# Other token widths in the last gate and the first mixer, and a one-instruction final scaling, in a two-layer hybrid trunk

## The chip, the cores and the metric

The kernel runs on one core of a Trainium2 chip. Its time is that of one execution on the device, in microseconds (us). The core's engines are named as in the profile: PE is TensorE (PEld is its weight loads, which overlap its products), DVE is VectorE, ACT is ScalarE, POOL is GpSimd, SP is SyncE, which issues nearly all DMAs. Every engine runs its instructions in order and waits on semaphores for what other engines produce.

## What is computed

The reference is one inference step of a trunk of two layers over 1024 prompt tokens and 8 sample tokens, 1032 in all, with 1024 features. Layer 0 mixes tokens with a convolution module, layer 1 with a chunked state-space scan; both have a feed-forward part and a gate:

```python
for i in range(DEPTH):
    u = rmsnorm(h, g_mix[i])
    o = conformer_mixer(u, ...) if i % 2 == 0 else mamba2_mixer(u, ...)
    h = h + o
    h = h + swiglu(rmsnorm(h, g_ffn[i]), ffn_w_gate[i], ffn_w_up[i], ffn_w_down[i])
    gate = jax.nn.sigmoid(rmsnorm(h, g_ple[i]) @ ple_w_gate[i])
    h = h + (p[i] @ ple_w_proj[i]) * gate
return rmsnorm(h, g_final), ...
```

The conformer mixer begins with `u @ w_pw1` (1024 x 2048), a sigmoid gate between its two halves, and a convolution over 31 tokens. The parts of interest here are that first product, at the kernel's start, and the second layer's `gate` with the final `rmsnorm`, at its end.

## The kernel before

Features lie on the 128 partitions, so that a tensor of 1024 features is 8 tiles `h[m]` of 128 x 1032 tokens. Every product is exact to about 32-bit: an operand is split into a high and a low part (`split`: ACT writes the high part in the matmul's fp32r type, DVE the difference), and one product of a 128-wide slice is three matmuls (`mm3`, lines 132 to 134), each with a weight load of its own. `product` (line 136) runs 8 slices, thus 24 matmuls, into one bank of PSUM. A bank holds 512 columns, so the 1032 tokens are cut into blocks, `BLK = ((0, 388), (388, 386), (774, 258))`, offset and width. PE has seven banks for such products (tag `mm`).

At the start, SP loads weights and inputs in an order written out by hand: the embedding's inputs `p` block by block (`ple_load`), the vectors, `x` block 0 (`load_x`), the weights of the first mixer product, then blocks 1 and 2 of `x`. PE first runs half of the embedding products of layer 0 (`ple_products`), meanwhile ACT and DVE split `x` (`ready`); then `pw1(m)` runs for each of 8 feature tiles two products per block, `a` and `b`. ACT copies the embedding products out of PSUM (`pstg`, line 250), which frees their banks.

At the end, `ple(1, ...)` runs the gate of layer 1 through `grouped`: tiles m = 0 and 1 for all three blocks, then tiles 2 to 7 for all three blocks, so that the weights of six tiles stay in place. After each product, `emit` does on DVE a multiplication by the norm factor (`t`, line 526), on ACT the sigmoid (527), on DVE a multiplication by the embedding product `pj` (528) and the addition to `h` (529), on ACT the square of `h` (204), on DVE its addition to `stat` (205). When a block has all 8 tiles, `norm.finish` sums over the partitions with a matmul (214, for the very last square 216), takes a root on ACT (219) and a reciprocal on DVE (220); then `after1` scales the 8 tiles by `g_final` and the norm factor and stores them. In blocks 0 and 1 a tile is scaled by ACT (line 1396) and then by POOL (1397); in the last block tiles 0, 2 and 4 likewise (1400, 1401) and the other five by one DVE instruction (1403). The last block's tiles are stored two by two, in four DMAs.

The order on each engine is not quite that of the code: a scheduler moves instructions within what their dependencies allow, when the program is built. Engines then follow that order.

Of the kernel before, what the change touches and what calls it, by code (L numbers as in the profile page):

```python
# [16 lines left out]
P = 128  # L17
# [8 lines left out]
NG = 8  # L26
PH = SEQ // 8 + 1
BLK = ((0, 388), (388, 386), (774, 258))
BLQ = tuple((T // 4 * b, T // 4) for b in range(4))
HT = T // 2  # L30
QT = T // 4
# [26 lines left out]
def trunk_kernel(ctx: ExitStack, tc: tile.TileContext, I, O):  # L58
# [172 lines left out]
                               op0=ALU.mult, op1=ALU.mult)  # L231
        split(t[:, :n], uh[:, o:o + n], ul[:, o:o + n], eng=eng)

    def ple_load(i, pt, stage, blocks=BLK, ks=(0, 1)):
        for o, n in blocks:
            for k in ks:
                raw = stage(k, o, n)
                nc.sync.dma_start(out=raw, in_=I["p"][i, k, :, o:o + n])
                split(raw, pt[k][0][:, o:o + n], pt[k][1][:, o:o + n])

    def ple_products(pool, ps, i, pt, tag, halves=(0, 1), w=None):
        for s in halves:
            w = w or kview(slab(I["w_proj"][i, s], 1024), 2)
            for mm in range(4):
                m = 4 * s + mm
                stg = pool.tile([P, T], F32, name="pstg", tag=tag, bufs=3 if tag == "v" else 2)
                for o, n in BLK:
                    a = ps.tile([P, 512], F32, name="a", tag="mm")
                    product(a[:, :n], w, mm * P, pt, o, n)
                    S.activation(out=stg[:, o:o + n], in_=a[:, :n], func=AF.Copy)  # L250
                nc.scalar.dma_start(out=proj_d[i][m], in_=stg)
                yield
            w = None
# [247 lines left out]
                    later(4, lambda o=o, n=n: norm.finish(o, n))  # L501
        return h, hs, u, norm.rstd

    def grouped(xp, weight, emit, after, cut=4):
        for ms in (range(cut), range(cut, KT)):
            ws = {}
            for o, n in BLK:
                for m in ms:
                    if o == 0:
                        ws[m] = kview(slab(weight(m), 1024, xp if m - ms[0] >= 2 else None, len(ms) - 2), KT)  # L510
                    emit(m, ws[m], o, n)
                    tick()
                if cut in ms:
                    after(o, n)

    def ple(i, h, nu, rstd2, ps, after):
        with tc.tile_pool(name=f"pleg{i}", bufs=2, reuse_waits="tile") as pool:
            norm = Norm(ps)

            def emit(m, w, o, n):  # L520
                pj = pool.tile([P, 388], F32, name="pj", tag="pj", bufs=3)
                nc.sync.dma_start(out=pj[:, :n], in_=proj_d[i][m, :, o:o + n])
                a = ps.tile([P, 512], F32, name="a", tag="mm")
                product(a[:, :n], w, 0, nu, o, n)
                t = pool.tile([P, 388], F32, name="t", tag="t", bufs=3)
                V.tensor_tensor(out=t[:, :n], in0=a[:, :n], in1=rstd2[:, o:o + n], op=ALU.mult)
                x = S.activation(out=t[:, :n], in_=t[:, :n], func=AF.Sigmoid)
                V.tensor_tensor(out=t[:, :n], in0=t[:, :n], in1=pj[:, :n], op=ALU.mult)
                V.tensor_tensor(out=h[m][:, o:o + n], in0=h[m][:, o:o + n], in1=t[:, :n], op=ALU.add)
                if o != BLK[-1][0] or m < KT - 1:  # L530
                    norm.add(h[m][:, o:o + n], o, n, V)
                else:
                    behind(S.activation(out=warm[:, :1], in_=warm[:, 1:], func=AF.Sqrt), x, norm.squared)
                    norm.add_last(h[m][:, o:o + n], n)

            def done(o, n):
                def run():
                    norm.finish(o, n)
                    after(norm.rstd, o, n)
                later(1, run)  # L540

            grouped(pool, lambda m: I["w_pgate"][i, m], emit, done, 2)

    l1a = None

# [7 lines left out]
    with tc.tile_pool(name="l0", bufs=2, reuse_waits="tile") as pool:  # L553
# [8 lines left out]
                norm.add(h[m][:, o:o + n], o, n, V)  # L562

        def ready(b):
            o, n = BLK[b]
            for m in range(KT):
                if b in SCALED_LATER:
                    split(h[m][:, o:o + n], U[m][0][:, o:o + n], U[m][1][:, o:o + n], scale=col("g_mix", m))
                else:
                    scaled_split(h[m], col("g_mix", m), norm.rstd, U[m], o, n)  # L570
# [4 lines left out]
        with tc.tile_pool(name="ple0", bufs=2, reuse_waits="tile") as pp:  # L575
            pt = [(pp.tile([P, T], F32R, name="ph", tag="ph"), pp.tile([P, T], F32R, name="pl", tag="pl"))
                  for _ in range(2)]
            praw = [pp.tile([P, T], F32, name="praw", tag="praw") for _ in range(2)]
            w0 = [wp.tile([P, 1024], F32, name="wraw", tag="wraw")] + \
                [pp.tile([P, 1024], F32R, name=f"w{x}", bufs=1) for x in "hl"]  # L580
            for k in range(2):
                hf = slice(512 * k, 512 * k + 512)
                nc.sync.dma_start(out=w0[0][:, hf], in_=I["w_proj"][0, 0, :, hf])
                split(*(t[:, hf] for t in w0))
                ple_load(0, pt, lambda k, o, n: praw[k][:, o:o + n], BLK[:1], (k,))
            ple_load(0, pt, lambda k, o, n: praw[k][:, o:o + n], BLK[1:])
            nc.sync.dma_start(out=vec, in_=I["vec"])
            load_x(*BLK[0])
            w1 = pw1_weights(0)
            for b in BLK[1:]:  # L590
                load_x(*b)
            for _ in ple_products(pp, ps, 0, pt, "pstg", (0,), kview(w0[1:], 2)):
                pass
            squares(*BLK[0])
            if 0 not in SCALED_LATER:
                norm.finish(*BLK[0])
            ready(0)

        cs = pool.tile([P, T], F32, name="cs", tag="cs", bufs=1)
# [4 lines left out]
        with tc.tile_pool(name="conv", bufs=2, reuse_waits="tile") as cp:  # L604
            def pw1(m, out, w=None):
                wa, wg = w or pw1_weights(m)
                v = cp.tile([P, T], F32, name="v", tag="v", bufs=3)
                out.append(v)
                for i, (o, n) in enumerate(BLK):
                    a = ps.tile([P, 512], F32, name="a", tag="mm")  # L610
                    product(a[:, :n], wa, 0, U, o, n)
                    b = ps.tile([P, 512], F32, name="b", tag="mm")
                    product(b[:, :n], wg, 0, U, o, n)
                    if i in SCALED_LATER:
                        r = norm.rstd[:, o:o + n]
                        s = pool.tile([P, 388], F32, name="s", tag="s")
                        V.tensor_tensor(out=s[:, :n], in0=b[:, :n], in1=r, op=ALU.mult)
                        t = pool.tile([P, 388], F32, name="t", tag="t")
                        V.tensor_tensor(out=t[:, :n], in0=a[:, :n], in1=r, op=ALU.mult)
                    else:  # L620
                        s, t = b, a
                    g = s if i in SCALED_LATER else pool.tile([P, 388], F32, name="s", tag="s")
                    S.activation(out=g[:, :n], in_=s[:, :n], func=AF.Sigmoid, bias=col("b_pw1", KT + m))
                    V.scalar_tensor_tensor(out=v[:, o:o + n], in0=t[:, :n], scalar=col("b_pw1", m), in1=g[:, :n],
                                           op0=ALU.add, op1=ALU.mult)
                    yield
# [77 lines left out]
            vs = []  # L704
            it = pw1(0, vs, w1)
            if 0 in SCALED_LATER:
                norm.finish(*BLK[0])
            for b in (1, 2):
                squares(*BLK[b])
                if b in SCALED_LATER:  # L710
                    ready(b)
                    next(it)
                    norm.finish(*BLK[b])
                else:
                    next(it)
                    norm.finish(*BLK[b])
                    ready(b)
            nc.sync.dma_start(out=st, in_=I["conv_state"])
            nc.sync.dma_start(out=cmask, in_=I["cmask"])
# [180 lines left out]
    def win(i):  # L900
        return kview(slab(I["w_in"][i], 1024), KT)

    ple(0, h, U, rstd, ps, after0)
    its = [in_proj(win(16 + ct), raw, cst[:, ct, :, 3], AF.Copy, 3) for ct, raw in zip((16, 24), raws)]
    for it in its:
        for _ in range(2):
# [444 lines left out]
    with tc.tile_pool(name="ps2", bufs=7, space=PSUM, reuse_waits="tile") as ps:  # L1351
# [35 lines left out]
        l1.close()  # L1387
        h, hp, u, rstd = ffn(1, entry, ps, xs)

        out = ctx.enter_context(tc.tile_pool(name="out", bufs=1)).tile([P, KT, BLK[-1][1]], F32, name="out")  # L1390

        def after1(rstd, o, n):
            for m in range(KT):
                hx, g, r = h[m][:, o:o + n], col("g_final", m), rstd[:, o:o + n]
                if o != BLK[-1][0]:
                    S.activation(out=hx, in_=hx, func=AF.Copy, scale=g)
                    G.tensor_tensor(out=hx, in0=hx, in1=r, op=ALU.mult)
                    nc.sync.dma_start(out=O["y"][m, :, o:o + n], in_=hx)
                elif m in (0, 2, 4):
                    S.activation(out=hx, in_=hx, func=AF.Copy, scale=g)  # L1400
                    G.tensor_tensor(out=out[:, m], in0=hx, in1=r, op=ALU.mult)
                else:
                    V.scalar_tensor_tensor(out=out[:, m], in0=hx, scalar=g, in1=r, op0=ALU.mult, op1=ALU.mult)
                if o == BLK[-1][0] and m % 2 == 1:
                    nc.sync.dma_start(out=O["y"][m - 1:m + 1, :, o:o + n].rearrange("m p n -> p m n"),
                                        in_=out[:, m - 1:m + 1])

        ple(1, h, u, rstd, ps, after1)
        flush()
        hp.close()  # L1410

# [125 lines left out]
```

## Time and profile before

| what | us |
|---|---|
| three runs | 3060.24, 3068.0, 3070.94 |
| their median | 3068.0 |
| the profiled execution | 3064.59 |
| its span, first to last instruction | 3062.8 |

The span is cut into times from its start. In the rows below, a timeline row gives an instruction's start, its duration, engine, line, what it writes and reads with partitions x columns, and in brackets how long its engine sat idle before it and what ended the idle time. A matmul's shown duration is longer than the distance to the next one, since matmuls are pipelined; what one costs PE is the distance between the starts.

### The profile page before, as it was taken

What the parts mean: (1) busy time and instruction counts of PE and PEld (TensorE: products, weight loads), DVE (VectorE), ACT (ScalarE), POOL (GpSimd) and SP (SyncE); (2) the same over time, 40 slices, a digit from 0 to 9 for tenths busy, and PEclk for the clock granted to TensorE, in tenths of its full rate; (3) what the DMA queues carried; (4) which work ended last, traced back from release to release, by engine and by line L of the source; (5) the groups of instructions that cost most, each with busy time, mean ns of one, the idle gap of its engine ahead of it and who ended that gap; (6) DMA issues with size and microseconds to landing.
All of it is one profiled execution on the core that took longest, in us unless ns stands there. A gap on an engine that the chain in (4) does not pass through costs nothing.

```text
span 3062.8 us, 51428 instructions
## 1 busy us (share of the span) xinstructions
PE 2933.8 (96%) x20613; PEld 2887.0 (94%) x20613; DVE 1971.8 (64%) x3206; ACT 1410.8 (46%) x2542; POOL 542.6 (18%) x540
## 2 busy tenths in 40 slices
PE   9999999999999999999999999999989999999997
PEld 8998889999999999899888998888889999999997
DVE  7787795555444478476687667865495555444476
ACT  6226653333321155666667676733353333321164
POOL 0001310000000021144454444531200000000022
PEclk9999999999999999999999999999999999999998
DMA  5336532222252233223334333566522222252222
GB/s 184 79 87 210 164 97 86 84 77 80 73 194 84 66 103 112 64 96 96 83 104 105 94 88 92 141 190 161 165 94 80 74 83 83 70 187 83 67 82 94
DMA packets 198063, 325.91 MB, mean 106 GB/s; under 512 B 50240, under 2 KB 120256, under 8 KB 197824
## 3 DMA queue, kind: packets, MB, share of 16 engines
q1 hardware_dynamic: 195520, 314.17, 33.4%
q10 hardware_dynamic: 2304, 8.46, 0.7%
q8 instruction: 162, 2.65, 0.4%
q14 instruction: 77, 0.63, 0.1%
HBM read 241.59 MB, written 72.58 MB: 103 GB/s over the span
## 4 chain that ended last, share of the span: by engine, by line
PE 73%; DVE 13%; ACT 6%; DMA 4%; issue 3%; POOL 1%; SPq 0%; DVEq 0%; ACTq 0%; POOLq 0%
PE a L134 8%; PE a L133 8%; PE a L132 8%; PE pA L132 5%; PE pA L133 5%; PE pA L134 5%; PE mm L133 4%; PE mm L132 4%; PE mm L134 4%; PE pC L134 3%; PE pC L132 3%; PE pC L133 3%; DVE xf L1024 2%; PE cacc L686 1%; PE pB L133 1%
## 5 line engine op out<-in xcount | busy, mean ns | idle before, releaser
L132 PE MATMUL mm<-u,whi 128*128 128x258 f32 (+2 forms) x1600 | 513.3, 322 | 13.5 <-ACT whi L112 8.8
L133 PE MATMUL mm<-u,whi 128*128 128x258 f32 (+2 forms) x1600 | 516.6, 323 | 0.5 <-DVE u L113 0.5
L134 PE MATMUL mm<-u,wlo 128*128 128x258 f32 (+2 forms) x1600 | 509.5, 320 | 1.6 <-DVE wlo L113 1.5
L112 ACT ACTIVATE whi<-wraw 128x1024 fp32r<-128x1024 f32 (+1 forms) x199 | 207.5, 1044 | 393.7 <-PE a L133 230.4
L205 POOL TENSOR_TENSOR stat<-stat,sq 128x258 f32<-128x258 f32 (+2 forms) x70 | 63.5, 907 | 1451.0 <-ACT sq L204 1445.4
L132 PEld LDWEIGHTS mm<-u,whi 128*128 128x128 f32 x1600 | 304.7, 191 | 16.4 <-ACT whi L112 9.8
L133 PE MATMUL a<-hh,whi 128*128 128x388 f32 (+2 forms) x984 | 316.0, 321 | 0.5 <-DVE hh L113 0.5
L134 PE MATMUL a<-hh,wlo 128*128 128x388 f32 (+2 forms) x984 | 315.6, 322 | 0.0
L132 PE MATMUL a<-hh,whi 128*128 128x388 f32 (+2 forms) x984 | 310.4, 322 | 4.3 <-ACT hh L112 4.3
L133 PEld LDWEIGHTS mm<-u,whi 128*128 128x128 f32 x1600 | 305.7, 191 | 2.6 <-DVE u L113 1.1
L134 PEld LDWEIGHTS mm<-u,wlo 128*128 128x128 f32 x1600 | 304.1, 191 | 3.9 <-DVE wlo L113 2.3
L113 DVE TENSOR_TENSOR wlo<-wraw,whi 128x1024 fp32r<-128x1024 f32 (+1 forms) x199 | 244.1, 1227 | 59.0 <-ACT whi L112 58.0
L474 DVE TENSOR_TENSOR h<-a,h 128x388 f32<-128x388 f32 (+2 forms) x288 | 145.5, 512 | 186.7 <-PE a L134 185.8
L132 PE MATMUL a<-u,whi 128*128 128x258 f32 (+2 forms) x648 | 205.1, 319 | 9.0 <-ACT u L112 6.6
L134 PE MATMUL a<-u,wlo 128*128 128x258 f32 (+2 forms) x648 | 200.8, 313 | 3.5 <-DVE wlo L113 3.5
L133 PE MATMUL a<-u,whi 128*128 128x258 f32 (+2 forms) x648 | 202.6, 314 | 0.0
L132 PEld LDWEIGHTS a<-hh,whi 128*128 128x128 f32 x984 | 185.3, 189 | 4.6 <-ACT hh L112 4.6
L133 PEld LDWEIGHTS a<-hh,whi 128*128 128x128 f32 x984 | 186.3, 189 | 0.8 <-DVE hh L113 0.8
L134 PEld LDWEIGHTS a<-hh,wlo 128*128 128x128 f32 x984 | 186.4, 189 | 0.1
L113 DVE TENSOR_TENSOR wal<-sa,wah 128x1024 fp32r<-128x1024 f32 x44 | 54.4, 1237 | 151.9 <-ACT wah L112 151.9
L132 PEld LDWEIGHTS a<-u,whi 128*128 128x128 f32 x648 | 123.4, 191 | 12.2 <-ACT u L112 7.6
L134 PEld LDWEIGHTS a<-u,wlo 128*128 128x128 f32 x648 | 123.4, 191 | 4.9 <-DVE wlo L113 4.7
(354 smaller groups left out, 8536.5 us busy)
## 6 DMA issues: line engine op xcount, KB each, us to landing
wraw<-in_w_in SPq DMA_DIRECT2D x48, 512.0 KB, 4.6
hid<-hid SPq DMA_DIRECT2D x88, 258.0 KB, 2.4
hraw<-hid SPq DMA_DIRECT2D x44, 516.0 KB, 3.6
wraw<-in_w_gate SPq DMA_DIRECT2D x44, 512.0 KB, 3.3
wraw<-in_w_up SPq DMA_DIRECT2D x44, 512.0 KB, 3.3
wraw<-in_w_pw SPq DMA_DIRECT2D x32, 512.0 KB, 3.5
wraw<-in_w_down SPq DMA_DIRECT2D x32, 512.0 KB, 3.5
am<-ac_d SPq DMA_DIRECT2D x64, 256.0 KB, 3.5
```

What stands on the lines that cost most here:

```text
L112: S.activation(out=hi, in_=raw, func=AF.Copy)
L113: eng.tensor_tensor(out=lo, in0=raw, in1=as32(hi), op=ALU.subtract)
L132: TE.matmul(out, lhsT=wh, rhs=xh, start=start, stop=False, skip_group_check=onto)
L133: TE.matmul(out, lhsT=wh, rhs=xl, start=False, stop=False, skip_group_check=onto)
L134: TE.matmul(out, lhsT=wl, rhs=xh, start=False, stop=stop, skip_group_check=onto)
L205: return eng.tensor_tensor(out=self.acc[:, o:o + n], in0=self.acc[:, o:o + n], in1=sq[:, :n], op=ALU.add)
L474: V.tensor_tensor(out=h[m][:, o:o + n], in0=a[:, :n], in1=h[m][:, o:o + n], op=ALU.add)
L686: TE.matmul(acc[:, j], lhsT=we[:, i], rhs=raw[:, g, 4 - e:132 - e], start=i == 0, stop=i == nb - 1)
L1024: V.scalar_tensor_tensor(out=d, in0=raw[:, j + o:j + o + 512], scalar=col("w_conv", 4 * ct + j), in1=d, op0=ALU.mult, op1=ALU.add)
```

## The change

A second and a third table of widths come beside `BLK`. `BLK0 = 258, 388, 386` is used for everything ahead of the convolution (loads of `x` and `p`, `ple_load`, `ple_products` of both layers, `ready`, `pw1`); `BLKF = 388, 386, 194, 64` for the gate of layer 1, which so has four blocks. In `after1`, all blocks but the last are scaled by one DVE instruction a tile; the last block, now 64 wide, is scaled and stored as before. `BLK` stays everywhere else.

```diff
 BLK = ((0, 388), (388, 386), (774, 258))
+BLK0 = ((0, 258), (258, 388), (646, 386))
+BLKF = ((0, 388), (388, 386), (774, 194), (968, 64))
...
-    def ple_load(i, pt, stage, blocks=BLK, ks=(0, 1)):
+    def ple_load(i, pt, stage, blocks=BLK0, ks=(0, 1)):
...
-                for o, n in BLK:
+                for o, n in BLK0:
                     a = ps.tile([P, 512], F32, name="a", tag="mm")
                     product(a[:, :n], w, mm * P, pt, o, n)
...
-    def grouped(xp, weight, emit, after, cut=4):
+    def grouped(xp, weight, emit, after, cut, blocks):
...
-                if o != BLK[-1][0] or m < KT - 1:
+                if o != blocks[-1][0] or m < KT - 1:
...
-            load_x(*BLK[0])
+            load_x(*BLK0[0])
...
-                for i, (o, n) in enumerate(BLK):
+                for i, (o, n) in enumerate(BLK0):
                     a = ps.tile([P, 512], F32, name="a", tag="mm")
                     product(a[:, :n], wa, 0, U, o, n)
...
-                if o != BLK[-1][0]:
-                    S.activation(out=hx, in_=hx, func=AF.Copy, scale=g)
-                    G.tensor_tensor(out=hx, in0=hx, in1=r, op=ALU.mult)
+                if o != BLKF[-1][0]:
+                    V.scalar_tensor_tensor(out=hx, in0=hx, scalar=g, in1=r, op0=ALU.mult, op1=ALU.mult)
                     nc.sync.dma_start(out=O["y"][m, :, o:o + n], in_=hx)
...
-        ple(1, h, u, rstd, ps, after1)
+        ple(1, h, u, rstd, ps, after1, BLKF)
```

The order moves at three places. First SP's queue at the start: the end of the first block of `x`, the two weight loads of the first mixer product, and the second block. Before:

```order
L558 DMA h_190<-in_x 128x388
L558 DMA h_191<-in_x 128x388
L558 DMA h_192<-in_x 128x388
L126 DMA wraw<-in_w_pw 128x1024 x2
L558 DMA h_185<-in_x 128x386
L558 DMA h_186<-in_x 128x386
```

and now:

```order
L560 DMA h_190<-in_x 128x258
L560 DMA h_191<-in_x 128x258
L560 DMA h_192<-in_x 128x258
L128 DMA wraw<-in_w_pw 128x1024 x2
L560 DMA h_185<-in_x 128x388
L560 DMA h_186<-in_x 128x388
```

The queue's order is the same; the first eight loads are narrower, and what is behind them starts that much sooner.

Second PE's last instructions: the end of the last tile's product, then the two matmuls of the last norm sum (`st`). Before:

```order
L132 MATMUL a<-u,xhi 128x258
L133 MATMUL a<-u,xhi 128x258
L134 MATMUL a<-u,xlo 128x258
L214 MATMUL st<-stat_28816,mean 128x258
L216 MATMUL st<-sq,mean 128x258
```

and now:

```order
L134 MATMUL a<-u,xhi 128x64
L135 MATMUL a<-u,xhi 128x64
L136 MATMUL a<-u,xlo 128x64
L216 MATMUL st<-stat_28816,mean 128x64
L218 MATMUL st<-sq,mean 128x64
```

Eight products of 24 matmuls at 258 columns are now eight at 194 and eight at 64, and a further norm sum, at 194 columns, stands after the 47th of the 64-wide matmuls of tiles 2 to 7.

Third DVE's queue in the block after the 386-wide one, around the reciprocal of that block's norm. Before, with the block's 258-wide evictions around it and the scaling on ACT and POOL:

```order
L529 TENSOR_TENSOR h_28825<-h_28825,t 128x258
L220 RECIPROCAL stat_28817<-stat_28817 128x386
L205 TENSOR_TENSOR stat_28816<-stat_28816,sq 128x258
L526 TENSOR_TENSOR t<-a,stat_28818 128x258
L528 TENSOR_TENSOR t<-t,pj 128x258
```

and now:

```order
L531 TENSOR_TENSOR h_28825<-h_28825,t 128x194
L222 RECIPROCAL stat_28817<-stat_28817 128x386
L207 TENSOR_TENSOR stat_28816<-stat_28816,sq 128x194
L528 TENSOR_TENSOR t<-a,stat_28818 128x194
L1398 SCALAR_TENSOR_TENSOR h_28822<-h_28822,vec,stat_28817 128x386
L1398 SCALAR_TENSOR_TENSOR h_28823<-h_28823,vec,stat_28817 128x386
L1398 SCALAR_TENSOR_TENSOR h_28824<-h_28824,vec,stat_28817 128x386
L1398 SCALAR_TENSOR_TENSOR h_28825<-h_28825,vec,stat_28817 128x386
L1398 SCALAR_TENSOR_TENSOR h_28826<-h_28826,vec,stat_28817 128x386
L1398 SCALAR_TENSOR_TENSOR h_28827<-h_28827,vec,stat_28817 128x386
L1398 SCALAR_TENSOR_TENSOR h_28828<-h_28828,vec,stat_28817 128x386
L1398 SCALAR_TENSOR_TENSOR h_28829<-h_28829,vec,stat_28817 128x386
```

Eight scalings stand in DVE's queue between one tile's `t` and its multiplication by `pj`; they stand so after the reciprocals of the 388-wide and the 194-wide block too.

## Rows read from the trace of the kernel before

**Rows 1.** The page's part 1: busy time, share and instructions of each engine.

```profile
PE 2933.8 (96%) x20613; PEld 2887.0 (94%) x20613; DVE 1971.8 (64%) x3206; ACT 1410.8 (46%) x2542; POOL 542.6 (18%) x540
```

**Rows 2.** Busy time by stretch: length, engines' busy us (instructions), granted clock, DMA, GB/s.

```profile
60.00:80.00 20.00, 20.00 (x148) 20.00 (x147) 19.99 (x39) 7.36 (x12) 0.03 (x1) 1.00 0.38 98
...
200.00:250.00 50.00, 50.00 (x355) 49.99 (x354) 38.06 (x70) 18.31 (x34) 0.12 (x1) 1.00 0.41 116
...
3020.00:3040.00 20.00, 20.00 (x148) 19.73 (x147) 14.04 (x24) 11.14 (x20) 3.91 (x5) 1.00 0.23 73
3040.00:3050.00 10.00, 5.13 (x39) 4.69 (x37) 8.88 (x12) 2.94 (x7) 8.02 (x7) 0.85 0.49 173
3050.00:3063.00 13.00, 1.73 (x4) 0.50 (x2) 6.11 (x8) 2.27 (x5) 2.72 (x3) 0.50 0.24 81
```

**Rows 3.** Timeline of PE in the last gate, some starts.

```profile
2950.44 0.34 PE L132 MATMUL a<-u,whi 128*128 128x388 f32 x1
...
2958.94 0.34 PE L132 MATMUL a<-u,whi 128*128 128x386 f32 x1
...
2967.40 0.60 PE L214 MATMUL st<-stat,mean 128*128 128x258 f32 x2
...
2967.95 0.28 PE L133 MATMUL a<-u,whi 128*128 128x258 f32 x1
...
2973.61 0.34 PE L132 MATMUL a<-u,whi 128*128 128x388 f32 x1
2973.79 0.33 PE L133 MATMUL a<-u,whi 128*128 128x388 f32 x1
2974.82 0.45 PE L134 MATMUL a<-u,wlo 128*128 128x388 f32 x1 [0.70 <-DVE wlo L113]
...
3044.12 0.28 PE L134 MATMUL a<-u,xlo 128*128 128x258 f32 x1
```

**Rows 4.** Timeline of weight loads: fp32r after a pause, then f32 with 32-column matmuls.

```profile
1247.14 0.19 PEld L133 LDWEIGHTS mm<-u,whi 128*128 128x128 f32 x1
1247.25 0.19 PEld L134 LDWEIGHTS mm<-u,wlo 128*128 128x128 f32 x1
...
2096.99 0.36 PEld L1224 LDWEIGHTS cb<-st,ones 128*128 128x128 f32 x2
2097.27 0.30 PEld L1134 LDWEIGHTS ys<-state,cf 128*128 128x128 f32 x2
```

**Rows 5.** Timeline of DVE and POOL ahead of the end.

```profile
3026.50 0.56 DVE L529 TENSOR_TENSOR h<-h,t 128x386 f32<-128x386 f32 x1
...
3034.69 0.43 DVE L529 TENSOR_TENSOR h<-h,t 128x258 f32<-128x258 f32 x1
3036.12 2.57 DVE L220 RECIPROCAL stat<-stat 128x386 f32<-128x386 f32 x1 [1.01 <-ACT stat L219]
...
3043.63 1.24 DVE L529 TENSOR_TENSOR h<-h,t 128x258 f32<-128x258 f32 x1
...
3038.77 9.25 POOL L1397 TENSOR_TENSOR h<-h,stat 128x386 f32<-128x386 f32 x8 [16.09 <-DVE stat L220]
```

**Rows 6.** The chain that ended last, and the last DMA issues of SP.

```profile
3049.13 0.43 DVE t L526
...
3050.02 0.95 ACT L533
...
3051.88 1.24 PE st L216 x2
...
3053.65 1.78 DVE stat L220
...
3056.55 3.31 SPq L1405 DMA_DIRECT2D out_y<-out  x4
```

**Rows 7.** Timeline of PE at the start: first products and its waits.

```profile
7.30 1.19 PE L132 MATMUL a<-ph,wh 128*128 128x388 f32 x2 [0.86 <-ACT ph L112]
...
26.68 0.45 PE L132 MATMUL b<-u,whi 128*128 128x388 f32 x1 [0.91 <-ACT pstg L250]
...
47.05 0.45 PE L132 MATMUL b<-u,whi 128*128 128x388 f32 x1 [0.67 <-ACT whi L112]
...
48.44 0.45 PE L134 MATMUL a<-u,wlo 128*128 128x388 f32 x1 [0.39 <-DVE wlo L113]
```

More of the change, by code (lines that the diff above doesn't have):

```diff
@@ L502, in ffn @@
         return h, hs, u, norm.rstd
-    def grouped(xp, weight, emit, after, cut=4):
+    def grouped(xp, weight, emit, after, cut, blocks):
         for ms in (range(cut), range(cut, KT)):
             ws = {}
-            for o, n in BLK:
+            for o, n in blocks:
                 for m in ms:
@@ L514, in grouped, with ple @@
                     after(o, n)
-    def ple(i, h, nu, rstd2, ps, after):
+    def ple(i, h, nu, rstd2, ps, after, blocks):
         with tc.tile_pool(name=f"pleg{i}", bufs=2, reuse_waits="tile") as pool:
@@ L540, in done @@
                 later(1, run)
-            grouped(pool, lambda m: I["w_pgate"][i, m], emit, done, 2)
+            grouped(pool, lambda m: I["w_pgate"][i, m], emit, done, 2, blocks)
     l1a = None
@@ L564, in ready @@
         def ready(b):
-            o, n = BLK[b]
+            o, n = BLK0[b]
             for m in range(KT):
@@ L584, in trunk_kernel @@
                 split(*(t[:, hf] for t in w0))
-                ple_load(0, pt, lambda k, o, n: praw[k][:, o:o + n], BLK[:1], (k,))
-            ple_load(0, pt, lambda k, o, n: praw[k][:, o:o + n], BLK[1:])
+                ple_load(0, pt, lambda k, o, n: praw[k][:, o:o + n], BLK0[:1], (k,))
+            ple_load(0, pt, lambda k, o, n: praw[k][:, o:o + n], BLK0[1:])
             nc.sync.dma_start(out=vec, in_=I["vec"])
-            load_x(*BLK[0])
+            load_x(*BLK0[0])
             w1 = pw1_weights(0)
-            for b in BLK[1:]:
+            for b in BLK0[1:]:
                 load_x(*b)
@@ L593, in trunk_kernel @@
                 pass
-            squares(*BLK[0])
+            squares(*BLK0[0])
             if 0 not in SCALED_LATER:
-                norm.finish(*BLK[0])
+                norm.finish(*BLK0[0])
             ready(0)
@@ L706, in trunk_kernel @@
             if 0 in SCALED_LATER:
-                norm.finish(*BLK[0])
+                norm.finish(*BLK0[0])
             for b in (1, 2):
-                squares(*BLK[b])
+                squares(*BLK0[b])
                 if b in SCALED_LATER:
@@ L712, in trunk_kernel @@
                     next(it)
-                    norm.finish(*BLK[b])
+                    norm.finish(*BLK0[b])
                 else:
                     next(it)
-                    norm.finish(*BLK[b])
+                    norm.finish(*BLK0[b])
                     ready(b)
@@ L901, in win @@
         return kview(slab(I["w_in"][i], 1024), KT)
-    ple(0, h, U, rstd, ps, after0)
+    ple(0, h, U, rstd, ps, after0, BLK)
     its = [in_proj(win(16 + ct), raw, cst[:, ct, :, 3], AF.Copy, 3) for ct, raw in zip((16, 24), raws)]
@@ L1388, in trunk_kernel @@
         h, hp, u, rstd = ffn(1, entry, ps, xs)
-        out = ctx.enter_context(tc.tile_pool(name="out", bufs=1)).tile([P, KT, BLK[-1][1]], F32, name="out")
+        out = ctx.enter_context(tc.tile_pool(name="out", bufs=1)).tile([P, KT, BLKF[-1][1]], F32, name="out")
         def after1(rstd, o, n):
@@ L1403, in after1 @@
                     V.scalar_tensor_tensor(out=out[:, m], in0=hx, scalar=g, in1=r, op0=ALU.mult, op1=ALU.mult)
-                if o == BLK[-1][0] and m % 2 == 1:
+                if o == BLKF[-1][0] and m % 2 == 1:
                     nc.sync.dma_start(out=O["y"][m - 1:m + 1, :, o:o + n].rearrange("m p n -> p m n"),
                                         in_=out[:, m - 1:m + 1])
-        ple(1, h, u, rstd, ps, after1)
+        ple(1, h, u, rstd, ps, after1, BLKF)
         flush()
```

## The prediction

> **What bounds the kernel now.** I read four views, in this order. First the busy times of the engines: PE is busy 96% of the span, DVE 64%, the others less [rows 1]. An edit therefore counts if it alters what PE has to do, or the two ends of the program where PE does not yet, or no longer, set the pace. Second the table by stretch: in 60 to 80 us and in 200 to 250 us PE has no idle time, nor in 3020 to 3040; from 3040 on it runs dry while DVE and POOL are still busy [rows 2]. So a time won or lost by PE in the first 60 us is passed on through the program, and the last 20 us belong to DVE and to a chain. Third PE's timeline in the last gate [rows 3] and at the start [rows 7], for the distance between starts and for PE's waits. Last the chain of waits at the end [rows 6].
>
> **PE in the last gate.** A product is 24 matmuls. With 388 columns 48 of them, two tiles, take 2958.94 - 2950.44 = 8.50 us, .177 us each; with 258 columns 47 take 2973.61 - 2967.95 = 5.66 us, .120 each [rows 3]. The line through both is .44 ns a column and some 7 ns: 194 columns would be .092 and 64 would be .035, if columns alone counted. They don't need to: there are as many weight loads as matmuls [rows 1], and each is of 128 columns whatever the product's width. Where PE starts after a pause, two fp32r loads stand .11 apart (1247.14 and 1247.25), and where matmuls of only 32 columns stand between, the second load of a pair at 2097.16 (2096.99 + .36, less the single load's .19) is followed by the next at 2097.27, again .11 [rows 4]. That is under .120, so at 258 columns the load is covered; at 194 and 64 it is not. I take .11 for both, because it is the only duration that the rows have for the part that doesn't shrink. The 8 tiles have 192 matmuls of 258 columns now, 192 x .120 = 23.1 us, and get 192 x (.11 + .11) = 42.2 us: **+19.1**. Bounds: by the line 192 x (.092 + .035 - .120) = +1.3; at .120 each, as if nothing shrank, +23.1; a dearer case is a rival below.
>
> The further norm sum at 194 columns costs by the columns of the one at 258, which held PE from 2967.40 to 2967.95 [rows 3], .55 less one matmul of .12: **+0.4**. The wait of .70 at 2974.82 for DVE's split of the weights, where the starts are 1.03 apart and .18 would do, goes: PE comes to it 4.8 us later (48 x .10, the first two tiles), while the weights and DVE's queue ahead of that split come no later: **-0.9**, at worst 0. PE's last product then ends at 3044.24 + 18.6 = 3062.9.
>
> Here the Trainium skill says two things. Its page "TensorE: Matmul & The Clock Gate", section "LDWEIGHTS (loading the stationary operand)", gives the columns divided by 1.2 as ns, 107 for 128 columns; it speaks against this change, and by it the term would be +18.0 in place of +19.1, so the rows agree.
>
> **The tail.** Now 18.6 us pass from the end of the last product (3044.24) to the end of the span. The first 4.9 are backlog: DVE reaches the last tile's `t` only at 3049.13 [rows 6], since the reciprocal of the 386-wide block took 2.57, and then operations of 258 columns took 1.24 while POOL worked on its 8 scalings (9.25 us from 3038.77), against .43 before [rows 5]. The change takes ACT and POOL out of these scalings and gives DVE 8 operations a block instead. Is DVE still late? By .56 at 386 and .43 at 258 columns [rows 5] an operation at 194 is .37 and at 64 is .23; a scaling of 386 columns I take at .6, just over .56. In the 194-wide stretch of tiles 2 to 7 DVE has 2.57 + 8 x .6 + 6 x 4 x .37 = 16.2 us, PE 144 x .11 = 15.8: even. In the 64-wide stretch it has the reciprocal at 194 (1.4 by 2.57 and 1.78), 8 x .37 and 24 x .23, thus 9.9 of 15.8, and the norm sum at 194 stands after the 47th matmul, 5.2 us in, so that its scalings are done 4 us before PE ends. The backlog goes but for some .2: **-4.7**. If DVE's operations stayed at 1.24 it would be late again; nothing on POOL is left there to make them so.
>
> The chain from 3049.13 to 3062.8 is 13.7 us. At 64 columns `t` is .23 rather than .43 (-.2), the two matmuls of the last norm sum, 1.24, cost by columns .3 to .5 (-.8), the reciprocal .6 rather than 1.78 (-1.2; 6.2 ns a column between the two rows); sigmoid, square and the first scaling, of which no row stands here, I count like DVE's operations, .2 to .4 each (-1.1). Table loads, semaphores and the four DMA issues of 3.31 [rows 6] don't shrink: **-3.3**, between -2 and -4.5. The last gate in sum: 18.6 - 4.7 - 3.3 = **+10.6**, between 9 (load at .107 and the tail at its best) and 16 (each at .120, the tail at its worst).
>
> **The start.** The first block of `p` is 258 wide, so its load and its split, for which PE waits .86 at 7.30, end a little sooner: -.3. The wait of .91 at 26.68 is for the eviction of a bank by ACT; the first three embedding products leave PE sooner, about half goes: -.5. The waits of .67 and .39 at 47.05 and 48.44 are for the split of a pair of weights [rows 7]; with three blocks of which the first is short, a wide product of the other weights stands in between, and they go at most: -1.1. Against it, the last block of pw1 is 386 rather than 258 wide, which makes its three last evictions .13 longer each: +.4; and PE reaches the second block of `x` some 4 us sooner, while DVE, which splits it, is busy all of 60 to 80 [rows 2]. No row says whether that split is ready; a wait of 2 us bounds it. I take **-1.5**, from -3 to +2. PE's own work is the same: the same widths in another order. The wider second block has its loads behind it in an unchanged queue of SP, with 130 columns less ahead.
>
> **Sum.** The profiled execution took 3064.59, span 3062.8; +10.6 - 1.5 = +9.1 gives 3073.7. It is 3.4 below the median of the three runs, 3068.0, on which a comparison rests: 3077.1, say **3077**. A measurement here tells about 0.3% from no change, 9.2 us, so this stands at that limit.
>
> **Rivals.** *The clock falls.* In 3040 to 3050, PE busy 5.13 of 10 us, the granted clock is .85, and then, nearly idle, .50 [rows 2], the lower of the two levels, 1.2 GHz. The array gets 64 columns in each .11 us of the last 15.8 us, a quarter of what it takes at the line's pace. If the clock falls there, loads at .21 make 144 x .10 = +14.4 more: 3077 + 15 = 3092. Against it: the loads keep PE at work throughout, and [rows 2] show the fall only with idle time.
>
> *Short fp32r matmuls lose their pace.* The trace has none below 258 columns. An f32 matmul of 258 columns holds PE .43 (above), 3.6 times the fp32r one. If short fp32r ones ran like this, 194 would be .32 and 64 at least .11: 192 x (.32 + .11 - .12) = +59, and +80 if its load also doubles; with the tail's -8 and the start about 3125 to 3145. No row speaks for it, none against.
>
> *Not slower: the load is hidden.* The .11 are distances between loads at a start, not in a steady row. If PE loads several weights ahead, columns alone count and PE gains +1.3 only. Then DVE is the bound: 16.2 us in the 194-wide stretch against 144 x .092 = 13.2, and the tail keeps 3 us of its backlog; the sum is about +1.3 + .4 - .9 + 3 - 8 - 1.5, thus -6 to, with half of the load hidden, +2: 3062 to 3070. It decides from the point where the two short matmuls together cost under .17, instead of .22. Nothing in 3020 to 3040, where loads are covered, speaks against it.
>
> The same page of the Trainium skill, section "Back-to-back issue gap", gives for a steady stream of loads and matmuls some 81 ns at 128 columns and a floor of 25 ns for 64; by these the short matmuls would not be held to .11, and with about .10 and .07 the PE term would be some +9 (an estimate from that page). No row here has a steady row of short matmuls to weigh it.
>
> *The start gives more.* If the stages behind the first mixer, which wait for SP and ACT, also come 4 us sooner, the start gives 6 us rather than 1.5: 3072, or slower by 4 if the second block isn't split in time.
>
> **Chances.** Forecast 57% (3071 to 3084, about half of it above 3077.2); lower clock 11%; fp32r pace 15%; load hidden 12%; start 5%. Slower by over 0.3%: 29 + 11 + 15 = 55%; within: 28 + 10 + 4 = 42%; faster: 3%. The range leaves out the fp32r case and what lies past the lower clock, and takes in most of the hidden load: 3066 to 3099.
>
> **What would show it.** In the trace of the changed kernel: the starts of 194- and 64-wide matmuls .11 apart (the forecast), .09 and .04 (hidden), .21 with a granted clock at half (clock), or .32 (fp32r); PE's last product at about 3061 to 3063; no operation over .6 us on DVE other than reciprocals after 3040; 10.6 us from there to the end; at 26, 47 and 48 us waits that are gone or half. It is wrong if the last gate's 194- and 64-wide products take under 33 or over 46 us in sum, or if PE waits again in the first 60 us by 2 us or more.

## The result, and the profile after

The changed kernel takes 3083.2 us (median of six runs, 3079.1 to 3084.3), the kernel before 3067.6 in the same count: the ratio is 1.0052, with an interval of 1.0042 to 1.0062. It is slower, by some 16 us. The forecast was 3077, its range 3066 to 3099.

The time is read best in three parts, with PE as the clock of the program: until PE starts the last gate (its first matmul of 388 columns there), the gate (to the end of its last product), and the tail (to the end of the span). The starts are those of timeline rows; the last matmul counts up to one more distance between starts. For the two profiled executions:

| part | before | after | moved |
|---|---|---|---|
| until the last gate | 2950.4 | 2947.0 | -3.4 |
| the last gate | 93.8 | 125.5 | +31.7 |
| the tail | 18.6 | 8.7 | -9.9 |
| span | 3062.8 | 3081.2 | +18.4 |

The table by stretch of the kernel after answers to [rows 2] (length; PE, PEld, DVE, ACT, POOL busy, with instructions; granted clock; DMA share, GB/s):

```profile
2950.00:2980.00 30.00, 30.00 (x190) 29.94 (x189) 20.79 (x38) 15.91 (x29) 1.99 (x3) 0.89 0.28 87
...
3020.00:3040.00 20.00, 20.00 (x146) 19.73 (x145) 14.44 (x28) 9.16 (x16) 0.00 (x0) 1.00 0.27 79
3040.00:3060.00 20.00, 20.00 (x148) 20.00 (x146) 15.76 (x47) 7.78 (x19) 0.00 (x0) 0.80 0.42 131
3060.00:3068.00 8.00, 8.00 (x39) 8.00 (x40) 1.13 (x5) 0.61 (x3) 0.00 (x0) 0.50 0.05 10
```

PE is busy all the time up to the last product, and DVE has plenty of room (15.8 of 20, then 1.1 of 8). But the granted clock is .80 and then .50, while PE is busy 8.00 of 8.00 us. Where it changes is seen in PE's timeline of the kernel after; each row is a start and a shown duration, and the distance between neighbouring starts is what a matmul costs:

```profile
2964.50 0.28 PE L135 MATMUL a<-u,whi 128*128 128x194 f32 x1
2964.61 0.28 PE L136 MATMUL a<-u,wlo 128*128 128x194 f32 x1
...
2970.02 0.28 PE L134 MATMUL a<-u,whi 128*128 128x64 f32 x1
2970.13 0.28 PE L135 MATMUL a<-u,whi 128*128 128x64 f32 x1
...
2973.84 0.40 PE L134 MATMUL a<-u,whi 128*128 128x64 f32 x1
2974.05 0.40 PE L135 MATMUL a<-u,whi 128*128 128x64 f32 x1
...
2977.51 0.53 PE L134 MATMUL a<-u,whi 128*128 128x388 f32 x1
2977.83 0.53 PE L135 MATMUL a<-u,whi 128*128 128x388 f32 x1
...
2980.42 0.34 PE L134 MATMUL a<-u,whi 128*128 128x388 f32 x1
2980.60 0.34 PE L135 MATMUL a<-u,whi 128*128 128x388 f32 x1
...
3071.90 0.40 PE L134 MATMUL a<-u,xhi 128*128 128x64 f32 x1
3072.11 0.40 PE L135 MATMUL a<-u,xhi 128*128 128x64 f32 x1
```

At 194 and at 64 columns the starts stand .11 apart, as forecast. Then, in the 64-wide products of the first two tiles, the distance doubles to .21, and so does that of the 388-wide matmuls behind them, .32 in place of .18, until 2980.4. The same happens in the 64-wide products of the last six tiles, from 3051.9 to the end. The level is 1.2 GHz, half of 2.4.

The end of the program answers to [rows 6]:

```profile
3072.77 0.23 DVE L528 TENSOR_TENSOR t<-a,stat 128x64 f32<-128x64 f32 x1 [3.54 <-PE a L136]
...
3075.00 0.69 PE L218 MATMUL st<-sq,mean 128*128 128x64 f32 x2 [1.79 <-ACT sq L211]
...
3076.07 0.55 DVE L222 RECIPROCAL stat<-stat 128x64 f32<-128x64 f32 x1 [2.27 <-ACT stat L221]
3076.66 1.29 DVE L1404 SCALAR_TENSOR_TENSOR out<-h,vec,stat 128x64 f32<-128x64 f32 x5
...
3077.15 1.93 SPq L1406 DMA_DIRECT2D out_y<-out  x4
```

DVE now waits for PE (3.54 us) where PE waited for DVE, so nothing is late at the end; the chain from the last product is 8.7 us. (Behind the 194-wide block's reciprocal, at 3053.27, the eight scalings stand a step later than the section on the change has it: between a tile's multiplication by `pj`, at 3054.84, and its addition, at 3057.63.)

### The profile page after: what moved, and what is told of

Its sections match the earlier page's. It is cut to its first block, busy times and chain, and to the rows that moved or that the text cites. A ratio compares the mean times of both kernels' runs of the same rounds, so it can differ in the third digit from the quotient of the medians.

```text
span 3081.2 us, 51907 instructions
## 1 busy us (share of the span) xinstructions
PE 2965.1 (96%) x20807; PEld 2920.9 (95%) x20807; DVE 1975.1 (64%) x3262; ACT 1409.3 (46%) x2545; POOL 520.4 (17%) x524
## 4 chain that ended last, share of the span: by engine, by line
PE 74%; DVE 13%; ACT 4%; DMA 4%; issue 2%; POOL 1%; SPq 1%; ACTq 0%; DVEq 0%; POOLq 0%
PE a L134 8%; PE a L136 8%; PE a L135 8%; PE pA L134 5%; PE pA L135 5%; PE pA L136 5%; PE mm L134 4%; PE mm L135 4%; PE mm L136 4%; PE pC L134 3%; PE pC L136 3%; PE pC L135 3%; DVE xf L1026 2%; PE pB L136 1%; PE pB L135 1%
## 5 line engine op out<-in xcount | busy, mean ns | idle before, releaser
L134 PE MATMUL a<-u,whi 128*128 128x258 f32 (+4 forms) x680 | 214.1, 317 | 7.3 <-ACT u L114 3.8
L136 PE MATMUL a<-u,wlo 128*128 128x258 f32 (+4 forms) x680 | 211.0, 312 | 3.0 <-DVE wlo L115 3.0
L135 PE MATMUL a<-u,whi 128*128 128x258 f32 (+4 forms) x680 | 212.5, 314 | 0.1
L134 PEld LDWEIGHTS a<-u,whi 128*128 128x128 f32 x680 | 131.1, 194 | 9.5 <-ACT u L114 4.5
L136 PEld LDWEIGHTS a<-u,wlo 128*128 128x128 f32 x680 | 130.9, 193 | 4.0 <-DVE wlo L115 3.8
```

The lines of the kernel that those rows point to most:

```text
L134: TE.matmul(out, lhsT=wh, rhs=xh, start=start, stop=False, skip_group_check=onto)
L135: TE.matmul(out, lhsT=wh, rhs=xl, start=False, stop=False, skip_group_check=onto)
L136: TE.matmul(out, lhsT=wl, rhs=xh, start=False, stop=stop, skip_group_check=onto)
```

## Experiments: the parts apart

Four kernels came first, each with a part undone or alone. The kernel before ran on the same chip with a median of 3070.1 us; ratios are to it.

**The last block undivided**, the other two parts as changed:

```diff
-BLKF = ((0, 388), (388, 386), (774, 194), (968, 64))
+BLKF = BLK
```

> The last block of the gate undivided again (258), all else as changed. Theory (the split costs 19 us of load-bound matmuls and, in the changed kernel's trace, some 13 us of lower granted clock; the DVE scaling and the start are gains): PE's last product ends some 31 us sooner, the chain behind it is again 13.7 us instead of 8.7, and DVE, which at the most has 17.2 us of work in the last 17.3 us of PE, is 0 to 2 us late. Time 3058 to 3061 us, 22 to 25 us under the changed kernel and 7 to 9 us under the one before. Rival (eight scalings in DVE's queue make it as late at the end as POOL's did): the 4.9 us of backlog stay, 3063 us or more.

Measured: 3059.2 us, ratio 0.9962 (0.9950 to 0.9975), thus 24 us under the changed kernel (28 by the ratios) and faster than the kernel before: the split alone makes the change slower. The gate takes 92.8 us, 32.7 less than in the changed kernel. The tail is 16.3 us; the chain behind the lateness is some 2 us shorter than the 13.7 I expected, since no wait is left between the two last norm sums (1.38 us before, for the last square); but the lateness of DVE is what the rival said, not the theory. That the time is still the theory's is due to that shorter chain and to a gate shorter by 32.7 us rather than 31, not to a DVE that keeps up. Rows of this kernel's last products and of the norm sum behind them:

```profile
3035.83 1.68 DVE L1398 SCALAR_TENSOR_TENSOR h<-h,vec,stat 128x386 f32<-128x386 f32 x3
...
3042.27 0.43 DVE L530 TENSOR_TENSOR t<-t,pj 128x258 f32<-128x258 f32 x1 [1.37 <-DMA pj<-proj]
...
3043.76 1.23 PE L216 MATMUL st<-stat,mean 128*128 128x258 f32 x2 [4.34 <-DVE stat L207]
```

PE has its last product behind it and waits 4.3 us for DVE, almost as long as before [rows 6]; the scalings run until 3037.4, two us before PE's last product ends, with evictions of three tiles still behind them in DVE's queue. Of the 4.3 us, 1.37 are DVE's own wait for a load of `pj`, which SP issues behind the stores of the scaled tiles.

**Only the scalings**:

```diff
-                    S.activation(out=hx, in_=hx, func=AF.Copy, scale=g)
-                    G.tensor_tensor(out=hx, in0=hx, in1=r, op=ALU.mult)
+                    V.scalar_tensor_tensor(out=hx, in0=hx, scalar=g, in1=r, op0=ALU.mult, op1=ALU.mult)
```

> Only the final scalings on DVE; widths all as before. Theory: without POOL at work no DVE operation of 258 columns takes 1.24 us, the backlog of 4.9 us goes but for 0 to 2 us; 3 to 5 us under the kernel before, 3063 to 3065. Rival (DVE is as late, since it takes over work of ACT and POOL): within 1 us of the kernel before.

Measured: 3065.9 us, ratio 0.9986 (0.9978 to 0.9995): 4 us under the kernel before, the size of the theory, but not by its way. The operations of 1.24 us are gone, as a row of this kernel's end against [rows 5] shows:

```profile
3044.97 0.42 DVE L530 TENSOR_TENSOR t<-t,pj 128x258 f32<-128x258 f32 x1
...
3051.25 1.23 PE L216 MATMUL st<-stat,mean 128*128 128x258 f32 x2 [4.28 <-DVE stat L207]
```

Yet PE waits 4.3 us for DVE here too: eight scalings of .54 in DVE's queue cost as much as the slower operations beside POOL did, with a wait for `pj` of 1.30 us among it. The gate is 92.8 us rather than 93.8, and the tail 16.4 rather than 18.6. The first of these comes from ACT, which I had left out. In the kernel before, ACT's scalings do not stand at the end alone; the scheduler puts them as early as a tile's square is done. Rows of ACT at the gate's start, before:

```profile
2967.98 0.62 ACT L1396 ACTIVATE h<-h,vec 128x386 f32<-128x386 f32 x1
2968.62 1.28 ACT L219 ACT_TABLE_LOAD   x1
2969.91 0.48 ACT L219 ACTIVATE stat<-st,eps 128x258 f32<-128x258 f32 x1
```

and with the scalings on DVE:

```profile
2970.38 0.53 ACT L203 ACTIVATE stat<-h 128x386 f32<-128x386 f32 x1 [1.23 <-DVE h L531]
2970.93 1.28 ACT L221 ACT_TABLE_LOAD   x1
2972.22 0.48 ACT L221 ACTIVATE stat<-st,eps 128x258 f32<-128x258 f32 x1
```

The root of the norm before the gate stands right behind the statistics, without a scaling of .62 between them. Behind that root wait the reciprocal, DVE's queue and with it the split of the weights, for which PE waits .70 at 2974.82 before [rows 3]. That wait is gone in both kernels with the scalings on DVE, and it is there, .70 at 2973.36, in the kernel with ACT's scalings that follows.

**Only the start**:

```diff
 BLK = ((0, 388), (388, 386), (774, 258))
+BLK0 = ((0, 258), (258, 388), (646, 386))
```

> Only the first mixer's widths 258/388/386; gate and scalings as before. Theory (the 3.4 us by which PE reaches the last gate sooner in the changed kernel's trace come from the start, 2.1 us, and from waits of the state-space stage that follow from it): 3.4 us under the kernel before, about 3064. Rival (only the first 2.1 us are the start's, the other 1.3 us differ from run to run): 3065.5. Rival of the prediction (the start gives nothing): 3067.6.

Measured: 3065.6 us, ratio 0.9984 (0.9975 to 0.9992), thus 2 to 8 us under the kernel before. The rival that the start gives nothing falls; the other two can't be told apart by the time. The traces say more. The first matmul of the convolution, which starts while the later tiles of `pw1` still run, by the view of its line (duration as minimum, median and maximum, first and last start), before and after:

```profile
L686 PE MATMUL cacc<-craw,we x384: 270/275/333, 70.6 to 256.7; 128*128 128x128 f32 x192
```

```profile
L688 PE MATMUL cacc<-craw,we x384: 270/275/319, 68.3 to 254.6; 128*128 128x128 f32 x192
```

Over all traces of this study it lies at 67.4 to 68.7 us in seven kernels with the new start, and at 70.1 to 70.9 in three with the old one: up to there the start is worth 2 to 3 us. What comes later scatters: PE reaches the last gate anywhere between 2946.4 and 2958.1 us in the seven with the new start, though their instructions between the first mixer and the gate stand in the same order, and at 2950.4 to 2956.4 in the three with the old. The 1.1 us more by which the changed kernel's profiled execution was ahead at the gate can't, from one trace, be given to the change. But the scatter does not hide everything. If gate and tail, as each kernel's trace has them, are taken off the median span of its runs (an estimate), PE reaches the gate at 2947 to 2952 us with the new start and at 2953 to 2956 with the old, some 5 us apart. So the start may be worth more at the gate than at 70 us, as this experiment's own 2 to 8 us say too; why isn't shown.

**Only the split**, with the scalings by ACT and POOL and the old start:

```diff
-BLK0 = ((0, 258), (258, 388), (646, 386))
+BLK0 = BLK
-                    V.scalar_tensor_tensor(out=hx, in0=hx, scalar=g, in1=r, op0=ALU.mult, op1=ALU.mult)
+                    S.activation(out=hx, in_=hx, func=AF.Copy, scale=g)
+                    G.tensor_tensor(out=hx, in0=hx, in1=r, op=ALU.mult)
```

> Only the last 258 tokens as 194 and 64; the other scalings by ACT and POOL and the start's widths as before. Theory: the last gate costs PE 19 us more by the load-bound matmuls and about 13 us more by the lower clock, the tail is 10 us shorter whoever scales, since PE now leaves DVE time enough: 3086 to 3088, some 3.4 us above the changed kernel. Rival (the shorter tail needs the scalings on DVE): 3090 or more, with DVE operations of over 0.6 us beside POOL in the 64-wide stretch.

Measured: 3095.7 us, ratio 1.0077 (1.0063 to 1.0090), 24 us above the kernel before. That is the rival's side, and partly by its mechanism: the tail is 8.6 us, as short as with DVE's scalings, so the theory holds there; but the gate is 3.2 us longer than in the changed kernel, 128.7. Beside POOL, DVE's operations of 194 columns take 1.17 us, DVE is late within the gate, and PE waits in the middle of its products:

```profile
3053.37 1.17 DVE L530 TENSOR_TENSOR t<-t,pj 128x194 f32<-128x194 f32 x1
...
3063.06 1.01 PE L216 MATMUL st<-stat,mean 128*128 128x194 f32 x2 [2.23 <-DVE stat L207]
...
3068.54 0.52 DVE L531 TENSOR_TENSOR h<-h,t 128x64 f32<-128x64 f32 x1
```

and POOL's scalings of the two blocks:

```profile
3051.11 8.64 POOL L1399 TENSOR_TENSOR h<-h,stat 128x386 f32<-128x386 f32 x8 [15.62 <-DVE stat L222]
3067.83 4.46 POOL L1399 TENSOR_TENSOR h<-h,stat 128x194 f32<-128x194 f32 x8 [8.08 <-DVE t L528]
```

So the scalings on DVE are worth some 3 us here as well, inside the gate rather than behind it. The difference to the changed kernel is 8 us by the ratios; the other 4 to 5 are the start and the scatter.

## Experiments: the clock, the load and the lateness

**Wide again.** The matmuls of the 64-wide block run over 194 columns, of which 130 are not read:

```diff
-                product(a[:, :n], w, 0, nu, o, n)
+                q = 130 if n == 64 else 0; product(a[:, :q + n], w, 0, nu, o - q, q + n)
...
-                V.tensor_tensor(out=t[:, :n], in0=a[:, :n], in1=rstd2[:, o:o + n], op=ALU.mult)
+                V.tensor_tensor(out=t[:, :n], in0=a[:, q:q + n], in1=rstd2[:, o:o + n], op=ALU.mult)
```

> The changed kernel, but the matmuls of its last block run over the last 194 columns and not 64; the 130 columns that are computed twice are not read, everything behind PE stays 64 wide. Both widths stand .11 us apart in the changed kernel at full clock, so at the same clock PE's time is the same. Theory (the clock falls because only 64 columns pass in each .11 us): granted clock 1.00 to the last product, the distances stay .11, PE ends some 13 us sooner; 13 us under the changed kernel, thus 2 to 4 us above the kernel before. Rival (the clock falls for another reason, such as a long row of load-bound matmuls, whatever their width): the distances go to .21 as in the changed kernel, and the time is that of the changed kernel, some 16 us above the one before.

Measured: 3074.9 us against 3069.5 of the kernel before on the same chip, ratio 1.0021 (1.0011 to 1.0031). Three times the columns make the kernel faster. The table by stretch and two rows of this kernel's PE at its end:

```profile
3050.00:3060.00 10.00, 10.00 (x92) 10.00 (x91) 8.21 (x27) 3.14 (x10) 0.00 (x0) 1.00 0.60 183
3060.00:3070.00 10.00, 10.00 (x91) 10.00 (x90) 7.07 (x25) 5.06 (x12) 0.00 (x0) 1.00 0.29 87
```

```profile
3070.59 0.28 PE L135 MATMUL a<-u,xhi 128*128 128x194 f32 x1
3070.71 0.28 PE L136 MATMUL a<-u,xlo 128*128 128x194 f32 x1
```

PE and PEld are as busy as in the changed kernel, 10.00 of 10; the granted clock is 1.00, the distances stay .11, and the gate takes 112.8 us in place of 125.5. The lower clock cost 12.7 us, and it was the few columns that brought it, not the row of loads. The time of the runs says 8 to 10 us; this execution reached the gate late, at 2958.1, within the scatter named above.

**130 and 128**:

```diff
-BLKF = ((0, 388), (388, 386), (774, 194), (968, 64))
+BLKF = ((0, 388), (388, 386), (774, 130), (904, 128))
```

> The changed kernel with the last 258 tokens as 130 and 128. Theory (a matmul below some 240 columns costs the .11 us of its weight load whatever its width): both stand .11 apart, PE's 384 matmuls take the 42 us of the changed kernel without its slow part, if the clock holds with 128 columns; the tail at 128 columns is 1 to 2 us longer than at 64: 4 to 6 us above the kernel before. Rival 1 (the clock falls here too): distances of .21, 15 us or more above the kernel before. Rival 2 (the .11 are of 194 and 64 alone, by chance): .07 apart at 130.

Measured: 3076.6 us, ratio 1.0023 (1.0014 to 1.0032), 7 us above the kernel before. Both widths stand .11 apart:

```profile
3048.18 0.28 PE L134 MATMUL a<-u,xhi 128*128 128x130 f32 x1
3048.29 0.27 PE L135 MATMUL a<-u,xhi 128*128 128x130 f32 x1
...
3065.15 0.27 PE L134 MATMUL a<-u,xhi 128*128 128x128 f32 x1
3065.26 0.27 PE L135 MATMUL a<-u,xhi 128*128 128x128 f32 x1
```

The clock holds to the last product, the gate takes 112.6 us and the tail 9.8, as the theory has it. With 64, 128, 130 and 194 columns at one and the same distance, the part that does not shrink is shown to be independent of the width up to 194. That it is the load is the reading that fits the distance of two loads [rows 4], though no run took the load away.

**388, 340 and 304**, with the last block undivided:

```diff
-BLKF = BLK
+BLKF = ((0, 388), (388, 340), (728, 304))
```

> The version with the last block undivided, its widths 388, 340 and 304 instead of 388, 386 and 258. In that version DVE was still late at the end by 4.3 us, with eight scalings of the middle block (4.35 us in all) and its reciprocal in its queue during the 17.3 us of PE's last products. Theory (DVE has too little time there): with 304 columns PE's last stretch is 144 x .140 = 20.2 us, DVE has 17.6 us of work in it, the lateness goes but for about 1 us, and the chain at 304 columns is 0.8 us longer: 2 to 3 us under the undivided version, 13 to 15 us under the kernel before. Rival (the lateness is a matter of order in DVE's or SP's queue, not of DVE's time): same or 1 us slower than the undivided version.

Measured: 3058.7 us, ratio 0.9970 (0.9959 to 0.9981), not to be told from the undivided version at 0.9962. In the trace the lateness goes, as the theory says: the norm sum stands right behind the last product without a wait, and the tail is 14.7 us rather than 16.3. The gate is .7 us shorter too. Of the 2 to 3 us that I expected, the trace shows 2.3; the runs scatter by more than that.

**No early scaling**: the undivided version with the scalings of the first two blocks left out, so that these are stored unscaled:

```diff
-                    V.scalar_tensor_tensor(out=hx, in0=hx, scalar=g, in1=r, op0=ALU.mult, op1=ALU.mult)
+                    pass
```

> The undivided version without the final scalings of its first two blocks (they are stored unscaled; the last block is scaled as before). Theory (the scalings make DVE late): the norm sum at the end no longer waits 4.3 us for DVE but under 1 us, the time is 3 to 4 us under the undivided version. Rival (SP's queue, whose stores stand ahead of the loads of pj, makes DVE late): a wait for pj of 1.4 us or more stays, and at most 2 us are won.

Measured: 3058.6 us, ratio 0.9968 (0.9956 to 0.9980), again the undivided version's time. The trace shows that the scalings make DVE late, as the theory says: the norm sum that waited 4.34 us has no wait, only the very last one for the chain:

```profile
3043.38 0.70 PE L216 MATMUL st<-stat,mean 128*128 128x258 f32 x2
...
3046.24 0.70 PE L218 MATMUL st<-sq,mean 128*128 128x258 f32 x2 [2.16 <-ACT sq L211]
```

The tail is 13.5 us, 2.8 less than with the scalings, where I expected 3 to 4; no wait for `pj` stays. But the stores no longer wait for a scaling either, so this run can't part the time that the scalings take in DVE's queue from the way through SP, where the loads of `pj` stand behind stores of scaled tiles. Both begin with the scalings.

## Why the prediction was right, and where it was off

**PE in the gate, +18.6.** Right. Without the slow clock (the wide-again version) the gate takes 112.8 us, 19.0 more than before. The .11 was measured as .112 at four widths. The bound by columns alone, +1.3, which stood behind the rival of the hidden load, is far off. So is the estimate of +9 from the Trainium skill's page "TensorE: Matmul & The Clock Gate", section "Back-to-back issue gap": its 81 ns at 128 columns stand against .112 us here, and its 25 ns at 64 are given there for a matmul by itself, not for one with a load. What the Trainium skill says of a load on the same page, in "LDWEIGHTS (loading the stationary operand)", 107 ns for 128 columns, agrees with the .112.

**The clock.** This is where 3077 became 3083. It stood as a rival at 11% and +15, with the sentence against it that the loads keep PE at work. That sentence failed: the clock fell with PE and PEld busy 8.00 of 8.00 us, and the wide-again version, with the same loads and more columns, kept it at 1.00. The rival had the mechanism and, within 2 us, the price: 12.7 against 14.4. The price is put together otherwise, though. The first 48 or so of the 144 last matmuls still ran at .11, so that these cost 9.6 and not 14.4; 3.1 more fall in the first two tiles, where the slow stretch reached into the 388-wide products behind it, of which I had not thought. By the rival's own sum the time would be 3092; that the result lies between is due to its price, to the tail and the start (below), and to the median.

**The wait of .70 in the gate, -0.9.** It went, and the reason given is enough: with the split alone, ACT's scalings in place, PE has no such wait either. But there is a second reason, not thought of, which is enough too: without the split it goes because ACT's scalings no longer stand in front of a root.

**The tail, -8.0.** Measured -9.9. The backlog went whole, -4.7 as put down: PE leaves DVE time, whoever scales, as the kernel with the split alone shows. The chain was mis-sized, -5.2 rather than -3.3. I held the four DMA issues of 3.31 for fixed, but they take 1.93 us: SP had been waiting for the scalings, whose row of five went from 3.49 to 1.29 us, and the end follows .8 us closer behind the last issue (2.1 us, before 2.9).

**DVE without POOL.** Right that nothing takes 1.24 any more. What the prediction did not weigh is that DVE's eight scalings in one row make the evictions as late as the contention did, as soon as PE does not leave room: with the last block undivided the lateness is 4.3 us.

**The start, -1.5.** At the first matmul of the convolution the traces give -2 to -3, inside its bounds. The runs of the start alone give -2 to -8 and the estimate above some -5, which is beyond them and near the rival of 6 us, which had 5%. The term was put too small; by how much, and whether for the rival's reason, stays open. The waits at 26.68, 47.05 and 48.44 [rows 7] are gone but for one of .92, now for the second half of a weight pair at 45.05; no wait for the second block of `x` came in.

**The signs put down.** The starts .11 apart came as forecast, and .21 with the clock at half as in the rival. The 194- and 64-wide products take 55 us in sum (12.2 and 42.8, with the norm sums between them), over the 46 above which the forecast was to be wrong, and PE's last product ends at 3072.5 rather than 3061 to 3063. So by the prediction's own sign its account of the gate failed, on the clock: in the wide-again version the same products take 44.0.

**The sum.** The forecast for the profiled execution was 3073.7 and it took 3083.1: 9.4 us more, of which 12.7 are the clock's, .4 PE's other work in the gate, less 1.9 in the tail and 1.9 until the gate. On the median 3.4 us were added, by which the profiled execution before lay below its own; the one after lies at its median, which takes these 3.4 off again and leaves the 6 us between 3077 and 3083. The sign and the main term were right. That 3083 still lies in the 3071 to 3084 that the forecast had without the lower clock is luck: 12.7 us of clock met 7 us of errors the other way, in the tail, the start and the median. Two sums beside the forecast don't come out: with its own terms (+59 or +80, the tail's -8, the start) the fp32r rival gives about 3117 to 3138, not 3125 to 3145, and the lower bound of the gate and tail together is about 8, not 9.

The undivided version is faster than both kernels, 3059.2 us: it keeps the new start and DVE's scalings and drops the split.

## What to carry to other kernels

A matmul that brings its own weights has a floor: here .11 us, from 64 to 194 columns. Cutting a block below the width at which the columns cover that (258 columns took .120) buys a shorter tail with PE time: against the undivided version 20 us, and 13 more by the clock, for a tail 8 us shorter. A PE that is busy all the time can still run at half its clock, so the granted clock of a stretch is read beside its busy time. And an operation moved to an engine with time to spare makes that engine late if it stands in one row ahead of what others wait for.

## What the runs showed of the hardware that was not expected

- The granted clock fell to half, with PE and its loads busy in the whole stretch, when 64 columns passed in each .11 us; with 128, 130 and 194 columns in the same .11 us it stayed at 1.00. Computing 130 columns for nothing so made the gate 12.7 us shorter.
- The slow level outlasts the narrow products: in the first two tiles the 388-wide matmuls behind them ran at .32 us, against .18, until 2980.4.
- Most of DVE's multiplications by `pj` and additions beside POOL's 386- and 388-wide scalings took 1.17 us at 194 columns, 1.24 at 258 and 1.38 at 386, against .36, .43 and .56: .81 or .82 more at every width. Beside POOL's 194-wide scalings two additions at 64 columns took .52 against .23, thus .29 more. In these rows the price goes with the width of POOL's operation and not of DVE's, so narrow operations suffer most in proportion. The operation that reads PSUM (`t`) kept its time, .41 at 258 columns.
